# A chunked RWKV-7 scan inside a projection stream: all its products on 64x64 weights, two visits per chunk

## The chip, the cores and the metric

The kernel runs on one core of one Trainium2 chip. The time is the device time of one execution in microseconds (us), the median of several runs. Busy times, waits and clocks come from one profiled execution, which has a time of its own.

## The reference

One layer of a decoder trunk is computed for a prompt of 512 tokens and for 8 sample tokens, 520 columns in all, with width 1024: a half-step SwiGLU, a mixing block with one input projection of 8448 columns, a second half-step SwiGLU, a gated input per layer and a final norm. The part that matters here is the time mixing of the prompt, a delta rule for each of 16 heads with a state of 64x64:

```python
def wkv_step(S, inp):
    r_t, decay_t, k_t, v_t, kk_t, b_t = inp
    sa = jnp.einsum('bhvk,bhk->bhv', S, kk_t)
    S = (S * decay_t[:, :, None, :]
         - sa[..., None] * b_t[:, :, None, :]
         + v_t[..., None] * k_t[:, :, None, :])
    y = jnp.einsum('bhvk,bhk->bhv', S, r_t)
    return S, y
...
z = h @ w_in          # r | k | v | loras | conv B, C, u | merge gates
S_new, ys = lax.scan(wkv_step, S0, (r, decay, k_mod, v, kk, kk * a))
y_A = groupnorm(ys) * gn_w + gn_b + bonus, times the gate
x = x + (sigmoid(g_A) * y_A + sigmoid(g_B) * y_B) @ w_out
```

## The kernel before, in words

Everything is float32. A projection is done as three products per 128x128 weight block (high part times high part, high times low, low times high); line 104 makes the high part of a loaded weight on ScalarE and line 105 the low part on VectorE. The tokens stand in two halves of 260 columns. In the mixing block these products are lines 525 to 527, before and after it lines 114 to 116; "big product" below means one of them.

The time mixing cuts the 512 tokens into 16 chunks of C = 32. For a pair of heads (128 partitions, 64 a head) `stage` makes the tiles AR (decayed keys and queries), BK, the masked scores W, and writes the transposed values into the lower 32 rows of each head's 64 rows of UV (line 772). `invert` inverts a chunk's triangular part in W and folds it into W's upper rows. `scan(q)` then carries the state S through the 16 chunks for two such pairs at once (e = 0 and 1), so it works on four heads; there are four scans, q = 0 to 3, and 64 chunk steps in all. One chunk step is:

- line 889: four products of the state with AR, one for each head, 64x64 weights, into the PSUM tile xy;
- line 894: four products of the values (lower 32 rows of UV) with 32x32 weights from W's lower rows, added to the upper rows of xy;
- line 897: VectorE copies the upper rows of xy into the upper rows of UV, twice 32x128;
- line 906: four products ds of UV with 64x64 weights, the state's increment;
- line 909: VectorE makes the next state from S, the decay lam and ds, two instructions;
- line 874 (`y_part`): four products with 32 columns of weights that complete the output rows of xy; they are issued in the next chunk's first visit, for the chunk before; lines 879 and 882 (`y_out`) then take the output out of PSUM on ScalarE.

A float32 product is two instructions in the trace, so four products are a group of eight records (x8), and each of the four lines has 512 of them. A head sits in partitions 0 to 63 or 64 to 127 (HP), and two products of different halves run side by side.

The chunk steps stand among the big products. A planner at the end of `mix` writes the program: every part is a Python generator, and each `yield a, b` says that a us of TensorE were issued and that b us have to pass before it goes on. Scans, inversions, stages and the output part `fin` take turns with the projections by this planner's clock. After that the framework orders each engine's instructions itself, by readiness, so a group of products need not stay together.

SyncE issues all DMA transfers from one queue, in order: the weights (`raw`, line 97, two buffers), the state out (`out_wkvp`, line 915) and the small tiles of the inversion. An entry that waits holds up those behind it.

Of the kernel before, what the change touches and what calls it, by code (L numbers as in the profile page):

```python
# [8 lines left out]
F32 = mybir.dt.float32  # L9
# [3 lines left out]
ALU = mybir.AluOpType  # L13
AX = mybir.AxisListType

P = 128
# [10 lines left out]
C = 32  # L27
NC = T // C
# [27 lines left out]
def hybrid_step(tc, I, O):  # L56
# [3 lines left out]
    with ExitStack() as top:  # L60
# [299 lines left out]
        with tc.tile_pool(name="mx", bufs=1) as mp:  # L360
            YS = []

            def ysplit(m):
                YS.append(pair(gp, m))
                split(YS, m, YM[m], ALL, nc.vector)
                X[m] = gp.tile([P, N], F32, tag=f"x{m}", name=f"x{m}")
                nc.sync.dma_start(X[m], xd[m])

            def wo_part():

                w = [wprep(I["wo"][m], NT, nc.vector) for m in range(2)]
                ps = [[mmps("wo"), mmps("wo")], [mmps("wo"), pp.tile([P, 512], F32, tag="xy", name="wo", bufs=2)]]
                for k in range(NT):
                    yield ("ys", k)
                    for i in range(2):
                        for j, cs in enumerate(HALF):
                            mm3(ps[i][j], w[i], k, k, YS, cs, k == 0, k == NT - 1)
                    yield 1.3, 0.0
                out.append(ps)

            out = []
            mix(tc, nc, mp, pp, dp, low0, wprep, mwps, mmps, V, VV, I, O, HS, YM, ysplit, wo_part,
                ident, pmask)
# [79 lines left out]
def mix(tc, nc, mp, pp, dp, low0, wprep, mwps, mmps, V, VV, I, O, HS, YM, ysplit, wo_part, ident, pmask):  # L463

    hh, hl = [a for a, _ in HS], [b for _, b in HS]
    v1, act, pool = nc.vector, nc.scalar, nc.gpsimd
# [4 lines left out]
    nc.sync.dma_start(sft, I["sft"])  # L471
    nc.sync.dma_start(cst8, I["cv0"])
    nc.sync.dma_start(smask, I["smask"])
    nsh = mp.tile([P, NZ, B + 1], F32, name="nsh")
    omm = mp.tile([P, NZ], F32, name="omm")
    hka = mp.tile([P, 4, NT], F32, name="hka")
# [19 lines left out]
    HP = (slice(0, 64), slice(64, 128))  # L496
# [5 lines left out]
    def wide(name, shape, bufs=2):  # L502
        return mp.tile([P] + shape, F32, tag=name, name=name, bufs=bufs)
# [129 lines left out]
    mid, both = {}, {}  # L633
# [34 lines left out]
    def stage(p):  # L668
# [39 lines left out]

        if p % 2 == 0:
            both[p // 2] = [wide(n, [NC, 2, 64]) for n in ("AR", "UV")]  # L710
        ar, uv = both[p // 2]
        AR, UV = ar[:, :, p % 2, :].rearrange("p c (s t) -> p c s t", s=2), uv[:, :, p % 2, :]
        W = wide("W", [NC, 128], 4)
# [5 lines left out]
        for cs, ps in zip(GROUPS, kps):  # L719
            for g in range(cs.start, cs.stop, GT):  # L720
                i = g // GT
                for h, hp in enumerate(HP):
                    nc.tensor.matmul(ps[hp, g - cs.start:g - cs.start + GT], rhs=ident[:GT, :GT], start=True, stop=True,
                                     lhsT=rs[:GT, 2 * i + h:2 * i + h + 1].broadcast_to([GT, 64]))
# [21 lines left out]

        dm = dp.tile([2, NC, C, CH], F32, tag="dm", name="dm", bufs=2)
        for h in range(2):
            for b in (0, CH):
                nc.sync.dma_start(dm[h, :, b:b + CH].rearrange("c j t -> j c t"), W[64 * h + b:64 * h + b + CH, :, b:b + CH])  # L750
        for s in range(2):
# [29 lines left out]
    Nz = mp.tile([P, NC, C], F32, name="Nz")  # L781
    pool.memset(F4, 0.0)
    pool.memset(Nz, 0.0)
    CH = C // 2
    UP = (slice(0, C), slice(64, 64 + C))

# [3 lines left out]
    def invert(p):  # L790
# [5 lines left out]
        df = dp.tile([2, NC, C, C], F32, tag="df", name="df", bufs=2)  # L796
        Mr = mp.tile([P, C, CH], F32, tag="Mr", name="Mr")
        for g in range(4):
            nc.sync.dma_start(Mr[32 * g:32 * g + 32], dm.rearrange("h c j t -> (h c) j t"))
        for h in range(2):  # L800
            nc.sync.dma_start(Nz[64 * h:64 * h + CH, :, CH:], W[64 * h:64 * h + CH, :, CH:C])
        yield 0.0, 3.0
        ft = mp.tile([P, 2, 4, CH], F32, tag="ft", name="ft")
        FB, MB = 4 * C + CH, CH * CH
# [51 lines left out]

    def scan(q):

        AR, UV = both[q]
        W, lam, _ = zip(st_out[2 * q], st_out[2 * q + 1])  # L860
        Y = AR
        S, prev = mp.tile([P, 2, 64], F32, tag="S", name="S", bufs=3), None
        pool.memset(S, 0.0)

        def at(ps, rows, e):
            return ps[rows, 64 * e:64 * e + 64]

        def cols(ps, rows):
            return ps[rows, 0:128].rearrange("p (e x) -> p e x", e=2)

        def y_part(c, xy):
            for e in range(2):
                for hp in HP:
                    nc.tensor.matmul(at(xy, slice(hp.start + C, hp.stop), e), lhsT=W[e][hp, c, C:64],  # L874
                                     rhs=UV[hp, c, e, :], start=False, stop=True, skip_group_check=True)

        def y_out(c, xy):
            if c % 2 == 0:
                act.activation(Y[:, c // 2], cols(xy, slice(0, P)), AF.Identity)
            else:  # L880
                for hp in HP:
                    act.activation(Y[hp.start:hp.start + C, c // 2], cols(xy, slice(hp.start + C, hp.stop)), AF.Identity)

        for c in range(NC):
            xy = pp.tile([P, 512], F32, tag="xy", name="xy", bufs=2)
            for e in range(2):

                for hp in HP:
                    nc.tensor.matmul(at(xy, hp, e), lhsT=AR[hp, c, e, :], rhs=S[hp, e, :], start=e == 0, stop=False,  # L889
                                     skip_group_check=True)  # L890
            for e in range(2):
                for h in range(2):
                    up, kp = slice(64 * h, 64 * h + C), slice(64 * h + C, 64 * h + 64)
                    nc.tensor.matmul(at(xy, up, e), lhsT=W[e][kp, c, 0:C], rhs=UV[kp, c, e, :], start=False, stop=True,  # L894
                                     skip_group_check=True)
            for up in (slice(0, C), slice(64, 64 + C)):
                v1.tensor_copy(UV[up, c], cols(xy, up))
            if c:
                y_part(c - 1, prev)
                y_out(c - 1, prev)  # L900
            prev = xy
            yield 0.76, 0.8
            ds = pp.tile([P, 512], F32, tag="us", name="ds")
            for e in range(2):
                for hp in HP:
                    nc.tensor.matmul(at(ds, hp, e), lhsT=W[e][hp, c, 64:], rhs=UV[hp, c, e, :], start=True, stop=True)  # L906
            S1 = mp.tile([P, 2, 64], F32, tag="S", name="S", bufs=3)
            for e in range(2):
                v1.scalar_tensor_tensor(S1[:, e, :], S[:, e, :], lam[e][:, c:c + 1], at(ds, slice(0, P), e),
                                        ALU.mult, ALU.add)  # L910
            S = S1
            yield 0.32, 0.8
        y_part(NC - 1, prev)
        y_out(NC - 1, prev)
        nc.sync.dma_start(O["wkvp"][2 * q:2 * q + 2].rearrange("q p v -> p q v"), S)
        yield 0.2, 0.5

# [116 lines left out]
    def ys(m):  # L1034
# [7 lines left out]
    LAG = 1.2  # L1042
    WIN, DENSE, LIGHT = 8.0, 5500, 0.3
    make = {"scan": scan, "invert": invert, "stage": stage, "fin": fin, "sample": lambda p: sample(),
            "rkv": rkv, "conv": conv, "gate": gate, "low": lowrank, "ys": ys, "wo": lambda p: wo_part()}
    each = lambda kind: [(kind, p) for p in range(NT)]
# [23 lines left out]
    while any(todo.values()) or any(bigs.values()) or live:  # L1070
# [12 lines left out]
        for row in (["big"] if thin and t > 4 else []) + list(todo):  # L1083
            c = live.get(row)
# [115 lines left out]
```

## Time and profile before

| | |
|---|---|
| time, median of 3 runs | 1581.4 us (1580.41 to 1581.67) |
| the profiled execution's own time | 1579.58 us |
| its span, first to last instruction | 1577.8 us |
| TensorE, VectorE, ScalarE, GpSimd busy | 1526.4, 898.7, 552.4, 227.5 us |
| the four scans, from the first product to the last | 78.2, 69.7, 77.5, 89.8 us |
| in them TensorE busy | 77.52, 69.70, 76.45, 84.44 us |
| in them VectorE busy | 54.12, 44.07, 54.17, 62.81 us |

A matmul's busy time overlaps the next one's, so a busy TensorE is not a TensorE at its peak. What a product takes of the engine's time is read from start to start: from the start of one row of the timeline to the start of the next.

### The profile page before, as it was taken

The numbers are of one execution on the slowest core, as the hardware profiler recorded it, in microseconds if no ns is written. First come the engines' busy times: TensorE is split into PE (matmuls) and PEld (weight loads), VectorE is DVE, ScalarE is ACT, GpSimd is POOL, SyncE is SP. The second block draws the span as 40 slices with busy tenths as digits, with TensorE's granted clock in tenths as the row PEclk, the third lists the DMA queues.
The fourth block names the chain that finished last, engine by engine and source line by source line (L and its number), as shares of the span: only waits on it lengthen the run. The fifth ranks groups of instructions, "written<-read, shape, count | busy, mean of one in ns | idle before, by whom it ended". The sixth has DMA issues, their size and how long they took to land. (4 is left out here: it accounts for less than half of the span.)

```text
span 1577.8 us, 35347 instructions
## 1 busy us (share of the span) xinstructions
PE 1526.4 (97%) x15252; PEld 1449.1 (92%) x15252; DVE 898.7 (57%) x1849; ACT 552.4 (35%) x920; POOL 227.5 (14%) x268
## 2 busy tenths in 40 slices
PE   7999999999989999999999998999999999999997
PEld 7999999999989887888887797789999999999997
DVE  7443334433698875757986667765554433443456
ACT  5222122232634342533443252244432212222343
POOL 3111001110222211201320103221011100111001
PEclk9999999999999999999999998999999999999998
DMA  6223222233322211212222221224222322223223
GB/s 206 86 90 108 88 86 91 86 131 116 108 78 74 79 50 47 78 44 60 74 68 56 71 70 64 99 78 150 88 87 94 109 92 72 90 94 120 95 84 105
DMA packets 77532, 140.68 MB, mean 89 GB/s; under 512 B 37512, under 2 KB 42632, under 8 KB 77376
## 3 DMA queue, kind: packets, MB, share of 16 engines
q1 hardware_dynamic: 77376, 138.43, 27.9%
q8 instruction: 119, 1.95, 0.5%
q14 instruction: 37, 0.30, 0.1%
HBM read 127.40 MB, written 10.74 MB: 88 GB/s over the span
## 5 line engine op out<-in xcount | busy, mean ns | idle before, releaser
L114 PE MATMUL big<-xh,hi 128*128 128x260 f32 x1632 | 462.8, 285 | 6.3 <-ACT hi L292 5.2
L115 PE MATMUL big<-xl,hi 128*128 128x260 f32 x1632 | 463.3, 284 | 2.9 <-DVE xl L160 2.9
L116 PE MATMUL big<-xh,lo 128*128 128x260 f32 x1632 | 462.7, 284 | 1.0 <-DVE lo L105 1.0
L104 ACT ACTIVATE hi<-raw 128x1024 fp32r<-128x1024 f32 (+1 forms) x203 | 225.2, 1110 | 624.1 <-PE big L115 292.5
L105 DVE TENSOR_TENSOR lo<-raw,hi 128x1024 fp32r<-128x1024 f32 (+1 forms) x202 | 265.3, 1314 | 98.5 <-ACT hi L104 96.8
L114 PEld LDWEIGHTS big<-xh,hi 128*128 128x128 f32 x1632 | 308.3, 189 | 7.0 <-ACT hi L292 5.2
L525 PE MATMUL big<-xh,hi 128*128 128x260 f32 x1040 | 311.2, 299 | 3.5 <-DVE cu L584 1.6
L115 PEld LDWEIGHTS big<-xl,hi 128*128 128x128 f32 x1632 | 309.0, 189 | 4.1 <-DVE xl L160 4.1
L116 PEld LDWEIGHTS big<-xh,lo 128*128 128x128 f32 x1632 | 308.6, 189 | 1.3 <-DVE lo L105 1.2
L527 PE MATMUL big<-xh,lo 128*128 128x260 f32 x1040 | 300.2, 289 | 2.8 <-DVE lo L105 2.8
L526 PE MATMUL big<-xl,hi 128*128 128x260 f32 x1040 | 301.3, 290 | 0.0
L525 PEld LDWEIGHTS big<-xh,hi 128*128 128x128 f32 x1040 | 197.9, 190 | 16.3 <-DVE k L542 1.6
L527 PEld LDWEIGHTS big<-xh,lo 128*128 128x128 f32 x1040 | 197.0, 190 | 7.4 <-DVE lo L105 3.4
L526 PEld LDWEIGHTS big<-xl,hi 128*128 128x128 f32 x1040 | 198.0, 190 | 5.0
L115 PE MATMUL big<-hl,hi 128*128 128x260 f32 x704 | 199.2, 283 | 1.9 <-POOL hl L249 1.9
L116 PE MATMUL big<-hh,lo 128*128 128x260 f32 x704 | 199.1, 283 | 0.0
L114 PE MATMUL big<-hh,hi 128*128 128x260 f32 x704 | 198.8, 282 | 0.0
L249 POOL TENSOR_TENSOR hl<-u,hh 128x520 fp32r<-128x520 f32 x44 | 70.3, 1599 | 608.2 <-ACT hh L248 608.2
L115 PEld LDWEIGHTS big<-hl,hi 128*128 128x128 f32 x704 | 132.5, 188 | 2.8 <-POOL hl L249 2.8
L114 PEld LDWEIGHTS big<-hh,hi 128*128 128x128 f32 x704 | 132.6, 188 | 0.0
L116 PEld LDWEIGHTS big<-hh,lo 128*128 128x128 f32 x704 | 132.6, 188 | 0.0
L244 DVE TENSOR_TENSOR u<-big,nR 128x260 f32<-128x260 f32 x88 | 37.6, 429 | 127.1 <-PE big L116 127.1
(257 smaller groups left out, 1779.8 us busy)
## 6 DMA issues: line engine op xcount, KB each, us to landing
raw<-in_win SPq DMA_DIRECT2D x66, 512.0 KB, 3.6
raw<-in_wu SPq DMA_DIRECT2D x44, 512.0 KB, 3.5
raw<-in_wd SPq DMA_DIRECT2D x32, 704.0 KB, 4.1
raw<-in_wg SPq DMA_DIRECT2D x43, 512.0 KB, 3.5
raw<-in_wo SPq DMA_DIRECT2D x8, 512.0 KB, 3.5
raw<-in_wpg SPq DMA_DIRECT2D x8, 512.0 KB
x<-in_xT SPq DMA_DIRECT2D x8, 260.0 KB, 5.6
xd<-x SPq DMA_DIRECT2D x8, 260.0 KB, 2.0
```

What stands on the lines that cost most here:

```text
L104: nc.scalar.activation(hi[:, :nk, :], raw[:, :nk, :], AF.Identity)
L105: lo_eng.tensor_tensor(lo[:, :nk, :], raw[:, :nk, :], hi[:, :nk, :].bitcast(F32), ALU.subtract)
L114: nc.tensor.matmul(ps[:, :HN], lhsT=hi[:, wk, :], rhs=x[k][0][:, cs], start=first, stop=False)
L115: nc.tensor.matmul(ps[:, :HN], lhsT=hi[:, wk, :], rhs=x[k][1][:, cs], start=False, stop=False)
L116: nc.tensor.matmul(ps[:, :HN], lhsT=lo[:, wk, :], rhs=x[k][0][:, cs], start=False, stop=last)
L244: nc.vector.tensor_tensor(u1[:, cs], ps, rr[0][:, cs], ALU.mult)
L249: nc.gpsimd.tensor_tensor(hl, u1, hh[:].bitcast(F32), ALU.subtract)
L525: nc.tensor.matmul(ps[:, :HN], lhsT=hi[:, k, :], rhs=hh[k][:, cs], start=k == 0, stop=False)
L526: nc.tensor.matmul(ps[:, :HN], lhsT=hi[:, k, :], rhs=hl[k][:, cs], start=False, stop=False)
L527: nc.tensor.matmul(ps[:, :HN], lhsT=lo[:, k, :], rhs=hh[k][:, cs], start=False, stop=k == nk - 1)
```

## The change

Three things are changed in the scan, and two that they need elsewhere.

```diff
@@ mix, once
+    for h in range(2):
+        v1.tensor_scalar(pmask[64 * h + C:64 * h + 64, C:64], pmask[64 * h + C:64 * h + 64, C:64], 0.5, None, ALU.mult)
@@ stage, once for two head pairs
         if p % 2 == 0:
             both[p // 2] = [wide(n, [NC, 2, 64]) for n in ("AR", "UV")]
+            for up in UP:
+                nc.sync.dma_start(both[p // 2][1][up].rearrange("p c e v -> p (c e v)"), zd)
@@ mix, once: a block of zeros in DRAM
+    zd = dp.tile([C, NC * 128], F32, name="zd")
+    for i in range(NC * 128 // 512):
+        nc.sync.dma_start(zd[:, i * 512:(i + 1) * 512], Nz[0:C].rearrange("p c j -> p (c j)"))
@@ scan
+        def behind(group):
+            for x in group[1:]:
+                tc.add_manual_dep(x.ins, group[0].ins.name, mybir.DependencyInfo(
+                    mybir.DependencyClass.NoSync, mybir.DependencyReason.DATA), reason="order")
         def y_part(c, xy):
-            for e in range(2):
-                for hp in HP:
-                    nc.tensor.matmul(at(xy, slice(hp.start + C, hp.stop), e), lhsT=W[e][hp, c, C:64],
-                                     rhs=UV[hp, c, e, :], start=False, stop=True, skip_group_check=True)
+            return [nc.tensor.matmul(at(xy, hp, e), lhsT=W[e][hp, c, 0:64], rhs=UV[hp, c, e, :], start=False, stop=True,
+                                     skip_group_check=True) for e in range(2) for hp in HP]
         for c in range(NC):
             xy = pp.tile([P, 512], F32, tag="xy", name="xy", bufs=2)
+            group = []
+            for e in (1, 0):
+                for hp in HP:
+                    group.append(nc.tensor.matmul(at(xy, hp, e), lhsT=AR[hp, c, e, :], rhs=S[hp, e, :], start=e == 1,
+                                                  stop=False, skip_group_check=True))
+            behind(group)
             for e in range(2):
                 for hp in HP:
-                    nc.tensor.matmul(at(xy, hp, e), lhsT=AR[hp, c, e, :], rhs=S[hp, e, :], start=e == 0, stop=False,
-                                     skip_group_check=True)
-            for e in range(2):
-                for h in range(2):
-                    up, kp = slice(64 * h, 64 * h + C), slice(64 * h + C, 64 * h + 64)
-                    nc.tensor.matmul(at(xy, up, e), lhsT=W[e][kp, c, 0:C], rhs=UV[kp, c, e, :], start=False, stop=True,
+                    nc.tensor.matmul(at(xy, hp, e), lhsT=W[e][hp, c, 0:64], rhs=UV[hp, c, e, :], start=False, stop=True,
                                      skip_group_check=True)
             for up in (slice(0, C), slice(64, 64 + C)):
                 v1.tensor_copy(UV[up, c], cols(xy, up))
-            if c:
-                y_part(c - 1, prev)
-                y_out(c - 1, prev)
-            prev = xy
-            yield 0.76, 0.8
+            yield 0.55, 0.8
             ds = pp.tile([P, 512], F32, tag="us", name="ds")
+            group = []
             for e in range(2):
-                for hp in HP:
-                    nc.tensor.matmul(at(ds, hp, e), lhsT=W[e][hp, c, 64:], rhs=UV[hp, c, e, :], start=True, stop=True)
+                for hp in HP[::-1]:
+                    group.append(nc.tensor.matmul(at(ds, hp, e), lhsT=W[e][hp, c, 64:], rhs=UV[hp, c, e, :],
+                                                  start=True, stop=True))
+            behind(group + y_part(c, xy))
...
-            yield 0.32, 0.8
-        y_part(NC - 1, prev)
-        y_out(NC - 1, prev)
+            y_out(c, xy)
+            yield 0.6, 0.8
```

The products of line 894 now take all 64 rows and 64 columns; the upper rows of UV are zero at that time (written once for each pair of head pairs by two DMA transfers), so those rows add nothing. The lower rows add to the output rows twice, there and in `y_part`, and the mask of that quarter is halved for it. `y_part` also takes 64 columns, and stands behind ds of its own chunk. `behind` lets no product of a group start before the group's first.

On TensorE, in the first scan, the order before. L889 and L894 make a chunk's first visit, L906 is ds; L525 to L527 are big products; rows are engine order, a trailing x2 is two alike in a row.

```order
L889 MATMUL xy<-S,AR 64x64 x2
L527 MATMUL big<-xh_4192,lo 128x260
L889 MATMUL xy<-S,AR 64x64 x2
L894 MATMUL xy<-UV,W 32x64 x4
L525 MATMUL big<-xh_4194,hi 128x260
L526 MATMUL big<-xl_4195,hi 128x260
L527 MATMUL big<-xh_4194,lo 128x260
L525 MATMUL big<-xh_4196,hi 128x260
L526 MATMUL big<-xl_4197,hi 128x260
L906 MATMUL ds<-UV,W 64x64
L527 MATMUL big<-xh_4196,lo 128x260
L906 MATMUL ds<-UV,W 64x64 x3
```

The state products and ds are each cut in two by a big product; L874's four follow the last row. At the same place of the changed program (L904 was 889, L910 was 894, L919 was 906, L887 was 874; L528 to L530 are the big products):

```order
L904 MATMUL xy<-S,AR 64x64 x4
L910 MATMUL xy<-UV,W 64x64 x4
L529 MATMUL big<-xl_4193,hi 128x260
L530 MATMUL big<-xh_4192,lo 128x260
L528 MATMUL big<-xh_4194,hi 128x260
L529 MATMUL big<-xl_4195,hi 128x260
L530 MATMUL big<-xh_4194,lo 128x260
L528 MATMUL big<-xh_4196,hi 128x260
L529 MATMUL big<-xl_4197,hi 128x260
L919 MATMUL ds<-UV,W 64x64 x4
L887 MATMUL xy<-UV,W 64x64 x4
```

Eight products stand together in each visit, and the output products are those of the same chunk.

On SyncE's queue, where the first scan ends, before: L799 loads a tile of the inversion, L97 a weight, L915 stores the state.

```order
L799 DMA Mr<-dm 32x512 [waits DMAHW1_49]
L97 DMA raw<-in_win 128x1024 [waits DMAHW2_49,DVE_49]
L915 DMA out_wkvp<-S 128x2x64 [waits DMAHW3_49,DVE_49]
L97 DMA raw<-in_win 128x1024 [waits DMAHW4_49,DVE_49]
L665 DMA wdi<-in_wdi 128x128 [waits DMAHW5_49,Pool_49]
```

The same place now:

```order
L97 DMA raw<-in_win 128x1024 [waits DVE_49]
L715 DMA UV<-zd 32x2048 [waits DMAHW3_49,DVE_49,PE_49]
L929 DMA out_wkvp<-S 128x2x64 [waits DMAHW4_49,DVE_49]
L715 DMA UV<-zd 32x2048 [waits DMAHW5_49]
L97 DMA raw<-in_win 128x1024 [waits DMAHW6_49,DVE_49]
```

The two transfers of zeros for the third scan's UV stand around the store of the first scan's state, and the first of them waits for TensorE.

## Rows read from the trace of the kernel before

**Rows 1.** Windows: us; PE, PEld, DVE, ACT, POOL busy (count); clock, DMA, GB/s.
```profile
555.40:633.60 78.20, 77.52 (x1064) 63.04 (x1063) 54.12 (x167) 25.29 (x59) 9.79 (x15) 1.00 0.19 54
942.50:1032.30 89.80, 84.44 (x1040) 68.26 (x1039) 62.81 (x138) 22.50 (x51) 25.46 (x24) 0.94 0.22 72
740.00:780.00 40.00, 37.38 (x398) 34.87 (x397) 37.20 (x103) 20.33 (x39) 12.54 (x16) 0.96 0.21 59
```

**Rows 2.** Timeline, TensorE, a whole chunk: start us, us, engine, line, tiles, count.
```profile
701.58 0.28 PE L527 MATMUL big<-xh,lo 128*128 128x260 f32 x1
701.79 0.45 PE L889 MATMUL xy<-S,AR 64*64 64x64 f32 x8
702.17 0.41 PE L894 MATMUL xy<-UV,W 32*32 32x64 f32 x8
702.51 0.41 PE L874 MATMUL xy<-UV,W 64*32 64x64 f32 x8
702.86 0.39 PE L525 MATMUL big<-xh,hi 128*128 128x260 f32 x1
703.08 0.28 PE L526 MATMUL big<-xl,hi 128*128 128x260 f32 x1
703.20 0.28 PE L527 MATMUL big<-xh,lo 128*128 128x260 f32 x1
...
704.12 0.45 PE L906 MATMUL ds<-UV,W 64*64 64x64 f32 x8
704.50 0.39 PE L525 MATMUL big<-xh,hi 128*128 128x260 f32 x1
```

**Rows 3.** Timeline, TensorE, a chunk cut in four, first scan.
```profile
586.05 0.28 PE L526 MATMUL big<-xl,hi 128*128 128x260 f32 x1
586.27 0.33 PE L889 MATMUL xy<-S,AR 64*64 64x64 f32 x4
586.53 0.38 PE L527 MATMUL big<-xh,lo 128*128 128x260 f32 x1
586.84 0.33 PE L889 MATMUL xy<-S,AR 64*64 64x64 f32 x4
587.10 0.41 PE L894 MATMUL xy<-UV,W 32*32 32x64 f32 x8
587.45 0.39 PE L525 MATMUL big<-xh,hi 128*128 128x260 f32 x1
...
588.03 0.28 PE L526 MATMUL big<-xl,hi 128*128 128x260 f32 x1
588.24 0.32 PE L906 MATMUL ds<-UV,W 64*64 64x64 f32 x2
588.50 0.39 PE L527 MATMUL big<-xh,lo 128*128 128x260 f32 x1
588.81 0.44 PE L906 MATMUL ds<-UV,W 64*64 64x64 f32 x6
589.18 0.41 PE L874 MATMUL xy<-UV,W 64*32 64x64 f32 x8
589.52 0.39 PE L525 MATMUL big<-xh,hi 128*128 128x260 f32 x1
```

**Rows 4.** Timeline, TensorE, 32 products on 64x64 weights in one visit.
```profile
812.89 2.08 PE L741 MATMUL sc<-AR,BK 64*64 64x64 f32 x64
814.90 0.39 PE L525 MATMUL big<-xh,hi 128*128 128x260 f32 x1
```

**Rows 5.** Groups by line: shape xcount | busy us, mean ns | idle before, releaser.
```profile
L897 DVE COPY UV<-xy 32x128 f32<-32x128 f32 x128 | 36.3, 283 | 46.1 <-PE xy L894 43.5
L906 PEld LDWEIGHTS ds<-UV,W 64*64 64x64 f32 x512 | 27.8, 133 | 15.9 <-DVE UV L897 2.4
L894 PEld LDWEIGHTS xy<-UV,W 32*32 32x32 f32 x512 | 16.3, 105 | 4.4
```

**Rows 6.** DMA issues: tile, queue, count, KB each, median us to landing.
```profile
raw<-in_win SPq DMA_DIRECT2D x66, 512.0 KB, 3.6
```

More of the change, by code (lines that the diff above doesn't have):

```diff
@@ L861, in scan @@
         Y = AR
-        S, prev = mp.tile([P, 2, 64], F32, tag="S", name="S", bufs=3), None
+        S = mp.tile([P, 2, 64], F32, tag="S", name="S", bufs=3)
         pool.memset(S, 0.0)
```

## The prediction

> **What bounds the kernel now.** I read first the page's busy shares, then a table of windows over the scans, then the timeline of TensorE around single chunks, and last the groups by line. The page has TensorE busy for nearly the whole span; since a matmul's busy time overlaps the next one's, the windows have to say whether it ever stood still. In the first scan it was busy 77.52 of 78.2 us [rows 1]: nothing that a scan waits for is seen there. Only the fourth scan has holes, 89.80 - 84.44 = 5.4 us, and a mean granted clock of 0.94, so part of it ran at the lower level. VectorE is busy 54.12 of 78.2 us in the first scan, 0.69, and 0.70 in the fourth. So what counts in a scan is what each visit takes of TensorE's time, and that is read from start to start.
>
> **What a visit takes.** The ordinary step from one big product to the next is 0.12 us (703.08 to 703.20) [rows 2]. From the last big product to the first one of a visit it is 0.21, that is 0.09 of entry; the first big product behind a visit holds 0.22, that is 0.10 of exit. Four products on 64x64 weights hold 0.38 (701.79 to 702.17, and again 704.12 to 704.50), four of line 894 hold 0.34 and four of line 874 0.35 [rows 2]. A whole chunk is then 0.09 + 0.38 + 0.34 + 0.35 + 0.10 = 1.26 for the first visit and 0.09 + 0.38 + 0.10 = 0.57 for the second, together 1.83 us.
>
> Many chunks are cut. State products cut 2 and 2: from 586.05 to 587.45 are 1.40 us, less two big steps 1.16, with the exit 1.26 [rows 3]; uncut, the two groups are 0.09 + 0.38 + 0.34 + 0.10 = 0.91. The cut costs 0.35. ds cut 1 and 3: from 588.03 to 589.52 are 1.49, less 0.24 and with the exit 1.35; uncut, ds and line 874 are 0.91. The cut costs 0.44: a single product holds nearly what two do, and each piece pays its entry, its exit and its own start and end.
>
> How often: I counted the program's order. Of 64 groups of state products 28 are cut, of 64 of ds 38; the scan's products stand in 209 runs, where two for each chunk would be 128. The 209 - 128 - 28 - 38 = 15 left over are groups of line 874 that stand alone, at 0.09 + 0.10 = 0.19 each. Before: 64 x 1.83 + 28 x 0.35 + 38 x 0.44 + 15 x 0.19 = 117.1 + 9.8 + 16.7 + 2.9 = 146.5 us of TensorE.
>
> **The changed visits.** No row has eight products in one visit, but 32 of one shape stand in one: they hold 814.90 - 812.89 = 2.01 us [rows 4]. From 4 to 32 products are 28 more for 2.01 - 0.38 = 1.63, so 0.058 each. Eight products hold 0.38 + 4 x 0.058 = 0.61, the visit 0.80 with entry and exit, the chunk 1.60. The bounds: if the two groups of a visit still paid for a change between them, a visit would be 0.91 as ds with line 874; nothing makes it less than 0.57 + 4 x 0.058. I take 0.80, as all eight have the same shape as those of rows 4. In the changed order there are 129 runs, and no state or ds group is cut; two of the others are. After: 128 x 0.80 = 102.4. Removed: 146.5 - 102.4 = **44 us**, of it 14.7 in whole chunks and 29 from the cuts. With 0.91 it would be 30.
>
> The wider weights cost something, and it is inside the 0.80. A load for line 894 has a mean of 105 ns, one for ds 133 [rows 5], 28 ns more for twice the columns; but the step from group to group grows only from 0.34 to 0.38 [rows 2], so a load is mostly hidden behind the product before it, and 128 groups lose 128 x 0.04 = 5 us. A rule of the Trainium skill speaks for more: "TensorE: Matmul & The Clock Gate", LDWEIGHTS, says that a weight load's time goes by its columns and not by its rows. The two means here agree in direction (28 ns for 32 more columns); what it would make of the time if loads set the pace is the third rival below.
>
> **What is added elsewhere**, all at nothing. Two small VectorE operations halve a mask at the start of the mixing block; by the nearest row, the 283 ns copy of the same 32 partitions [rows 5], they would be 0.6 us uncovered; the big products that open the block hide them. Twelve DMA transfers: four write 64 KB of zeros each, eight bring 256 KB into UV. A weight of 512 KB lands in 3.6 us [rows 6] with the DMA engines at 0.19 to 0.22 in the scans [rows 1]. They are on SyncE's queue. Those for the third and the fourth scan wait until TensorE has read UV for the last time in the scan two before; behind them stand weight loads. But they stand beside the store of that scan's last state, which waited for the same chunk and held up the same loads before. The work that hides them is the weight already in the other buffer, 48 big products or 48 x 0.12 = 5.8 us. With that cover gone they cost two late loads, 2 x 3.6 = 7 us. VectorE's and ScalarE's instructions in the scan stay the same in number; the last output products now come with their own chunk.
>
> **What comes back as waits.** A scan is shorter by 11 us in the mean and VectorE has the same work in it: 54.12 us in 78.2 - 11, or 0.81; 62.81 in 89.8 - 11, or 0.80. Each visit waits for VectorE: the second for the two copies (2 x 283 ns), the first for the two halves of the state. Behind a waiting product on TensorE's queue stand the big products, so each wait counts in full. Also, line 874's 0.34 us no longer stand between line 894 and ds, as a cover for the copies. From below: the fourth scan's 5.4 us of holes go. From above: the window 740 to 780, where VectorE is busy 37.20 of 40 us, 0.93, and TensorE lost 40.00 - 37.38 = 2.6 us, or 6.5% [rows 1]; over the four scans, 315 - 44 = 271 us, that is 18 us. The first scan at 0.69 lost 0.7 of 78.2, or 0.9%. A share of 0.81 lies about halfway, but the nearer row is the one at 0.69, and the chunk's steps are spaced as before (nine big products, 1.1 us, between most visits): I take 2%, or 6 us.
>
> **The sum**, against the profiled execution's own 1579.6: 1579.6 - 44 + 6 = 1541.6. The runs' median, 1581.4, lies 1.8 above that execution: **1543 us**. The likeliest case's own range is 1533 to 1554.
>
> **Rivals.**
> *VectorE becomes the bound* of the scans, so that most of the cuts' price only hid its work. For: 0.93 in the window 740 to 780, and more scans than one at 0.8 afterwards. Against: VectorE itself waits 43.5 us for line 894 before its copies [rows 5], so it is more often early than late. It gives back 18 us by the row above, or the whole visits come out at 0.91: 1581.4 - 44 + 18 = 1555, 1581.4 - 30 + 18 = 1569. 1555 to 1570.
> *More than the sum*: the holes of the fourth scan go, and the stretch at the lower clock with them. At 0.94 over 89.8 us the clock was at its lower level, half, for about 2 x 0.06 x 89.8 = 11 us, which cost 5. 1581.4 - 44 - 5 - 5 = 1527. Against: that scan runs beside the sample tokens' state work, which the change leaves where it is.
> *Weight loads set the pace.* As a mechanism of this kernel: each of the 1024 loads of lines 894 and 874 takes 28 ns more [rows 5], and the next product waits for it. 1024 x 0.028 = 29 us, of which 5 are counted: 1543 + 24 = 1567. The 0.34 and 0.38 of rows 2 are against it.
> *Slower: VectorE's queue.* Place: line 897's copies and line 909's updates behind other VectorE work. If at each of the 128 visits one more of its instructions stood ahead (the window 740 to 780 has 37.20 us for 103 of them, 0.36 each [rows 1]) and TensorE had no slack, 46 us would come back, and the time would be level, 1581.4 - 44 + 46 = 1583; with one at the first visits and two at the second, 69 us: 1606. It decides from 44 / 128 = 0.34 us of added wait in the mean. Against: the first scan, where such instructions stood ahead too, lost 0.7 us in 32 visits.
> *The change not doing what it says* is out as far as the order goes: 129 runs.
>
> **Chances.** The forecast 0.62 (1533 to 1554), VectorE the bound 0.20, more than the sum 0.10, weight loads 0.04, slower 0.04. A change of 0.2%, 3 us, is about what this kernel's runs can tell from none. Faster 0.95, the same 0.02, slower 0.03. The range for 8 in 10 is 1530 to 1562: it takes in the likeliest case, half of VectorE as the bound and a part of the case above the sum.
>
> **What would show it.** Visits of eight products that step 0.61 from their first start to the next big product; big products still 0.12; 64 x 2 visits. If a row of the timeline splits in a visit at the change from line 904 to 910, the drain between them was not saved. Scans of about 66, 62, 66 and 75 us; VectorE at 0.8 in them. Waits of lines 919 and 904 for VectorE by a few us together, of big products for a late weight by none. The forecast is wrong if TensorE's holes in the scans are above 15 us, or if a visit holds 0.9.

## The result and the profile after

The changed kernel takes 1537.95 us, the median of 4 runs (1536.35 to 1539.6), beside 1581.54 for the kernel before (1580.41 to 1583.73): ratio 0.9723, 95% interval 0.9706 to 0.974, or 44 us less. The forecast was 1543, with a range of 1530 to 1562.

The first window table of the changed kernel answers [rows 1]: its four scans, then the mixing block in two parts, from the first scan's start to the fourth's, and from there to the block's last big product. The columns are those of [rows 1].

```profile
557.80:622.00 64.20, 63.62 (x1049) 56.31 (x1048) 53.16 (x170) 24.92 (x58) 8.74 (x15) 1.00 0.23 61
661.40:722.80 61.40, 61.33 (x871) 54.95 (x872) 44.19 (x113) 19.30 (x45) 7.79 (x17) 1.00 0.20 59
819.80:883.30 63.50, 62.96 (x1047) 55.81 (x1048) 50.93 (x168) 24.25 (x55) 10.30 (x14) 1.00 0.24 66
916.70:989.40 72.70, 66.23 (x840) 58.34 (x839) 61.68 (x135) 20.22 (x47) 24.72 (x22) 0.95 0.27 90
557.80:916.70 358.90, 348.25 (x5113) 317.83 (x5112) 276.39 (x779) 160.94 (x334) 62.02 (x101) 0.99 0.26 71
916.70:1043.10 126.40, 119.93 (x1330) 111.28 (x1330) 95.54 (x211) 45.28 (x88) 32.91 (x34) 0.97 0.27 88
```

The same two parts of the kernel before:

```profile
555.40:942.50 387.10, 376.62 (x4931) 326.83 (x4930) 277.49 (x779) 158.04 (x329) 59.15 (x100) 1.00 0.23 63
942.50:1086.30 143.80, 136.51 (x1513) 119.37 (x1513) 96.06 (x212) 48.04 (x92) 33.50 (x35) 0.96 0.24 78
```

The first part is 28.2 us shorter, the second 17.4, together 45.6; the first scan starts 2.4 us later (557.8 against 555.4); behind the block both kernels run the same 491.5 us. TensorE stood still (window less busy) for 10.5 + 7.3 = 17.8 us before and for 10.6 + 6.5 = 17.1 now. So nearly all of the gain is time that TensorE was held, and none of it came back as waits. VectorE is busy 0.83 of the first scan and 0.85 of the fourth, where it was 0.69 and 0.70, with nearly the same work in them.

The later start is TensorE's clock. The stretch from 420 us to the first scan, before and now:

```profile
420.00:555.40 135.40, 124.95 (x1496) 118.94 (x1494) 112.85 (x268) 59.13 (x120) 33.17 (x60) 0.99 0.29 81
420.00:557.80 137.80, 128.85 (x1496) 123.00 (x1494) 112.67 (x268) 59.02 (x120) 33.97 (x60) 0.95 0.32 89
```

TensorE has the same 1496 records there and stands still for less (9.0 us against 10.5), but it is busy 3.9 us longer, at a mean granted clock of 0.95 instead of 0.99. In e8 below, which writes no zeros, the clock of this stretch is 0.96 and the scan starts at 557.2, so the zeros are not needed for it; what made the clock fall stays open.

One chunk's first visit in the second scan and the copies and loads, by the timeline and the groups by line, which answer [rows 2] and [rows 5]:

```profile
700.05 0.28 PE L530 MATMUL big<-xh,lo 128*128 128x260 f32 x1
700.26 0.45 PE L904 MATMUL xy<-S,AR 64*64 64x64 f32 x8
700.54 0.40 PE L910 MATMUL xy<-UV,W 64*64 64x64 f32 x8
700.87 0.39 PE L528 MATMUL big<-xh,hi 128*128 128x260 f32 x1
701.10 0.28 PE L529 MATMUL big<-xl,hi 128*128 128x260 f32 x1
```

```profile
L913 DVE COPY UV<-xy 32x128 f32<-32x128 f32 x128 | 36.0, 282 | 31.2 <-PE xy L910 29.8
L910 PEld LDWEIGHTS xy<-UV,W 64*64 64x64 f32 x512 | 21.0, 136 | 0.1
```

The visit holds 700.87 - 700.26 = 0.61 between its edges, as forecast; the step between the two groups is 0.28 where it was 0.38. The exit is 701.10 - 700.87 - 0.12 = 0.11, so the whole visit is 0.81. A load of line 910 takes 136 ns, where one of line 894 took 105, and the visit is as short as forecast all the same. VectorE still waits 29.8 us for line 910 (43.5 before), so it is still early more often than late.

For the experiments I summed, over all 2048 records of the scan's products, the steps from each start to the next start on TensorE, with entries and exits; what a step had above 0.35 us was counted as waiting. This is what the scan *holds*: 149.0 us before, 104.7 after, 44.3 less. How an entry or an exit beside another small product is counted can move one sum by 1 to 2 us and a difference of two by about 1. Beside it stand the runs of scan products in each program's order, the groups of state products and of ds that are cut in it, and what TensorE stood still in the two parts of the block, with the second part's granted clock.

| kernel | runs | cut | ratio (95%) | holds | still, 1st + 2nd part | clock |
|---|---|---|---|---|---|---|
| before | 209 | 28, 38 | 1 | 149.0 | 10.5 + 7.3 | 0.96 |
| after | 129 | 0, 0 | 0.9723 (0.9706 to 0.9740) | 104.7 | 10.6 + 6.5 | 0.97 |
| e1 before, kept together | 131 | 1, 1 | 0.9873 (0.9855 to 0.9891) | 120.0 | 13.0 + 9.9 | 0.93 |
| e2 after, first ready | 180 | 24, 29 | 0.9833 (0.9812 to 0.9854) | 126.4 | 11.5 + 4.3 | 0.97 |
| e3 values on 32 rows | 128 | 0, 0 | 0.9748 (0.9727 to 0.9768) | 111.8 | 9.7 + 6.2 | 0.99 |
| e4 outputs on 32 columns | 129 | 1, 0 | 0.9819 (0.9804 to 0.9834) | 112.1 | 9.5 + 12.2 | 0.94 |
| e5 outputs in next visit | 137 | 2, 1 | 0.9745 (0.9721 to 0.9769) | 109.8 | 10.4 + 7.5 | 0.95 |
| e6 copies twice | 124 | 0, 0 | 0.9858 (0.9837 to 0.9879) | 107.7 | 14.2 + 16.3 | 0.90 |
| e7 planned 0.8 | 131 | 0, 1 | 0.9745 (0.9727 to 0.9764) | 106.9 | 12.2 + 6.6 | 0.96 |
| e8 as e3, no zeros | 128 | 0, 0 | 0.9769 (0.9747 to 0.9790) | 113.0 | 9.9 + 6.1 | 0.96 |
| e9 one operation on GpSimd | 129 | 0, 0 | 0.9710 (0.9690 to 0.9730) | 103.8 | 10.6 + 7.3 | 0.99 |
| e10 as e4, three scans | 131 | 1, 0 | 0.9737 (0.9719 to 0.9755) | 109.1 | 9.7 + 5.5 | 0.99 |
| e11 two on GpSimd | 129 | 0, 0 | 0.9754 (0.9734 to 0.9773) | 105.6 | 10.8 + 13.4 | 0.97 |
| e12 after again | 129 | 0, 0 | 0.9706 (0.9685 to 0.9727) | 104.2 | 10.9 + 6.2 | 0.99 |

The kernel before took 1584 to 1585 us beside e1 to e12, so they are compared by their ratios; 0.001 is 1.6 us.

### The profile page after: what moved, and what is told of

Same layout as the page of the kernel before. It is cut to its first block, busy times and chain, and to the rows that moved or that the text cites. A ratio compares the mean times of both kernels' runs of the same rounds, so it can differ in the third digit from the quotient of the medians.

```text
span 1534.6 us, 35437 instructions
## 1 busy us (share of the span) xinstructions
PE 1484.7 (97%) x15252; PEld 1435.5 (94%) x15252; DVE 897.3 (58%) x1851; ACT 552.5 (36%) x920; POOL 230.9 (15%) x269
## 4 chain that ended last, share of the span: by engine, by line
PE 47%; DVE 5%; issue 2%; ACT 1%; POOL 1%; DMA 0%; DVEq 0%; POOLq 0%; ACTq 0%; SPq 0%
PE big L115 10%; PE big L114 10%; PE big L116 10%; PE big L528 4%; PE big L530 4%; PE big L529 4%; PE xy L904 1%; PE ds L919 1%; DVE lo L105 1%; PE xy L910 1%; PE xy L887 1%; PE sc L746 0%; DVE fo L457 0%; PE ft L856 0%; ACT hi L104 0%
## 5 line engine op out<-in xcount | busy, mean ns | idle before, releaser
L528 PE MATMUL big<-xh,hi 128*128 128x260 f32 x1040 | 310.3, 298 | 1.7 <-ACT cc L580 1.0
L530 PE MATMUL big<-xh,lo 128*128 128x260 f32 x1040 | 299.6, 289 | 2.0 <-DVE lo L105 2.0
L528 PEld LDWEIGHTS big<-xh,hi 128*128 128x128 f32 x1040 | 199.8, 192 | 11.4 <-ACT cc L580 1.2
L530 PEld LDWEIGHTS big<-xh,lo 128*128 128x128 f32 x1040 | 199.2, 192 | 4.2 <-DVE lo L105 2.3
```

The costliest lines, as they stand in the source:

```text
L528: nc.tensor.matmul(ps[:, :HN], lhsT=hi[:, k, :], rhs=hh[k][:, cs], start=k == 0, stop=False)
L530: nc.tensor.matmul(ps[:, :HN], lhsT=lo[:, k, :], rhs=hh[k][:, cs], start=False, stop=k == nk - 1)
```

## The experiments

**Cuts alone.** e1 is the kernel before with the changed order inside a group:

```diff
-            for e in range(2):
+            group = []
+            for e in (1, 0):
                 for hp in HP:
-                    nc.tensor.matmul(at(xy, hp, e), lhsT=AR[hp, c, e, :], rhs=S[hp, e, :], start=e == 0, ...)
+                    group.append(nc.tensor.matmul(at(xy, hp, e), lhsT=AR[hp, c, e, :], rhs=S[hp, e, :], start=e == 1, ...))
...
-                for hp in HP:
-                    nc.tensor.matmul(at(ds, hp, e), ...)
+                for hp in HP[::-1]:
+                    group.append(nc.tensor.matmul(at(ds, hp, e), ...))
+            behind(group)
```

(The first visit's group also takes in the products of the values and the output products; that is left out here.)

> The kernel before, with its narrow weights and its output products in the next chunk's first visit, but with the order that keeps a visit together: the group that needs two VectorE results begins with the product that needs the last one. In its order 131 runs of scan products instead of 209, 1 group of state products and 1 of ds cut instead of 28 and 38. If the cuts cost what the prediction's working says (28 x 0.35 + 38 x 0.44 + 15 x 0.19 = 29 us): 1581.5 - 29 = 1552. If a cut only moved waiting time about, so that what is saved comes back as waits for VectorE: 1570 or above. If all of the gain is the shapes': 1581.

Measured 1564.9, ratio 0.9873, 20 us less. The scan holds 29.0 us less, as expected, but 9 came back by the runs, and 12 in the profiled executions, where the block takes 513.7 us instead of 530.9. TensorE stands still 2.5 us longer in the first part and 2.6 in the second, and the clock fell to 0.99 and 0.93. The lower level is half of the upper one, so a window in which TensorE works all the time loses its length times what its mean clock lacks to 1. As an estimate from these rows that is 0.07 x 140.3 - 0.04 x 143.8 = 4 us more in the second part, and up to 4 (0.01 x 373.4) in the first. Its two parts:

```profile
553.80:927.20 373.40, 360.40 (x4929) 320.09 (x4928) 277.56 (x779) 158.19 (x329) 58.81 (x100) 0.99 0.23 65
927.20:1067.50 140.30, 130.40 (x1513) 118.03 (x1513) 96.90 (x211) 48.12 (x92) 33.58 (x35) 0.93 0.25 80
```

The cuts are most of the price (29 of the 44 us), and what their absence gives may come back in part.

**The old order in the new shapes.** e2 is the changed kernel with the order turned back, `behind` kept:

```diff
-            for e in (1, 0):
+            for e in range(2):
...
-                for hp in HP[::-1]:
+                for hp in HP:
```

> The changed kernel with the products of a group in the old order (e = 0 and the lower half first), the groups' added dependencies kept. In its order 180 runs, 24 groups of state products and 29 of ds are cut again; shapes, zeros and the place of the output products as changed. If the cuts are what costs: 24 x 0.35 + 29 x 0.44 = 21 us back, 1538 + 21 = 1559. If the change of shapes is what brought the time: 1538 to 1543.

Measured 0.9833, 17 to 20 us above the changed kernel; the scan holds 21.7 more, as expected. One of its cuts in the timeline: a single ds product holds 580.91 - 580.66 = 0.25, and the other three the rest of their visit.

```profile
580.45 0.28 PE L530 MATMUL big<-xh,lo 128*128 128x260 f32 x1
580.66 0.33 PE L919 MATMUL ds<-UV,W 64*64 64x64 f32 x2
580.91 0.39 PE L528 MATMUL big<-xh,hi 128*128 128x260 f32 x1
581.23 0.38 PE L919 MATMUL ds<-UV,W 64*64 64x64 f32 x5
```

So `behind` doesn't keep a visit whole. The changed program without it has the same order on every engine, row for row (so it wasn't run), and with it the old order is cut all the same. What keeps it whole is which product stands first, since that is all that e2 changes: now it is the one that needs VectorE's last result. The reason is read from the program and not measured: the group then becomes ready all at once; before, the first product was ready one VectorE instruction ahead of the rest and was put in.

**Rows and columns.** e3 gives the products of the values 32 rows and 64 columns, e4 the output products 64 rows and 32 columns; e10 is e4 in the first three scans alone.

```diff
# e3
-                    nc.tensor.matmul(at(xy, hp, e), lhsT=W[e][hp, c, 0:64], rhs=UV[hp, c, e, :], ...)
+                    kp = slice(hp.start + C, hp.stop)
+                    nc.tensor.matmul(at(xy, hp, e), lhsT=W[e][kp, c, 0:64], rhs=UV[kp, c, e, :], ...)
# e4 (e10: n = C if q < 3 else 0)
-            return [nc.tensor.matmul(at(xy, hp, e), lhsT=W[e][hp, c, 0:64], ...
+            return [nc.tensor.matmul(at(xy, slice(hp.start + C, hp.stop), e), lhsT=W[e][hp, c, C:64], ...
```

> The changed kernel with the products of the values on 32 rows and 64 columns of weights instead of 64 and 64; the zeros are then not needed, but still written; visits stay together (128 runs). If any change of shape inside a visit has the engine drained: the first visit holds 0.91 instead of 0.81, 64 x 0.10 = 6.5 us, 1544.5. If only a change of the columns does: first visits at 0.81 and 1538, and the 64 rows and zeros were not needed.

> The changed kernel with the output products on 64 rows and 32 columns of weights, behind ds in its visit as now. If any change of shape drains: the second visit holds 0.91 instead of 0.81, 64 x 0.10 = 6.5 us, 1544.5. If only a change of the rows does: 1538. With the kernel of 32 rows and 64 columns it tells apart which of the two numbers counts.

> The kernel with output products on 32 columns (ratio 0.982, 8 us more than the drain's price), but only in the first three scans; the fourth has the changed kernel's 64x64. If the drain's price is right, 0.10 at each of 48 second visits, and the rest came from VectorE's lateness beside the sample tokens in the fourth scan: 4.8 us above the changed kernel, ratio 0.9755. If a change of columns costs more than its rows show wherever it stands: three quarters of 15, 11 us above, ratio 0.979.

Both hold 7 us more (111.8 and 112.1 against 104.7). A visit of each, with its step from group to group 0.38 instead of 0.28, e3 first:

```profile
705.63 0.45 PE L904 MATMUL xy<-S,AR 64*64 64x64 f32 x8
706.01 0.45 PE L911 MATMUL xy<-UV,W 32*64 32x64 f32 x8
706.38 0.39 PE L528 MATMUL big<-xh,hi 128*128 128x260 f32 x1
```

```profile
703.58 0.45 PE L919 MATMUL ds<-UV,W 64*64 64x64 f32 x8
703.96 0.41 PE L887 MATMUL xy<-UV,W 64*32 64x64 f32 x8
704.30 0.39 PE L528 MATMUL big<-xh,hi 128*128 128x260 f32 x1
```

Either number changing costs the step, so the zeros and the 64 rows are needed. The Trainium skill has the rule, "TensorEngine Tiling (Array Packing)", Key Properties: "Changing tiling mode (not just tile) drains the TensorE". These rows agree and put about 0.1 us to it.

e3 came out 4 to 7 us above the changed kernel, as expected, e4 15 to 18. The fourth scan's part of e4 and the longest waits of TensorE in it (engine, line, waited for: us, times, longest) say more:

```profile
925.90:1063.20 137.30, 125.15 (x1330) 114.91 (x1330) 97.71 (x211) 41.76 (x84) 32.22 (x34) 0.94 0.24 80
```

```profile
PE ds L919 <- DVE UV L913: 5.7, 4, 1.6
...
PE big L530 <- DVE lo L105: 5.1, 3, 4.0
```

VectorE had fallen behind there. This part is 10.9 us longer than the changed kernel's: 4.6 of them in the fourth scan (925.9 to 1003.2, 77.3 us against 72.7) and 6.3 behind its last product, where at 1006.6 one weight's low part came 4.0 us late. e10, with the same price in three scans and the changed kernel's products in the fourth, holds 4.9 us more than e12, for 4.8 expected. Its ratio is 0.0031 or 4.9 us above e12's, but only 0.0014 or 2.2 us above the changed kernel's first one, so the time agrees with the price without fixing it. e4's other 8 to 11 us go with the narrow output products in the fourth scan; which of the changes in the order they come from isn't shown.

**The place of the output products.** e5 puts them back into the next chunk's first visit, on 64x64 weights:

```diff
+            if c:
+                group += y_part(c - 1, prev)
+                y_out(c - 1, prev)
+            behind(group)
```

> The changed kernel with the output products back in the next chunk's first visit, as 64x64 weights: a visit of twelve and one of four products instead of eight and eight. In its order 137 runs, 4 groups of all kinds cut. By the price of a visit nothing changes: first visits 0.80 + 4 x 0.058 = 1.03, second ones 0.57, together 1.60, four runs more at 0.19 and the cuts 2 us: 1540. If the place of the output products behind ds is what saves time (a cover for the state's update, or the output leaving PSUM earlier), it is slower by 5 us or more: 1543 or above.

Measured 1543.1, 0.9745, 4 to 6 us above, of it 5 in what the scan holds: its 8 additional runs and its cuts, more than the 2 us expected. Standing still is 17.8 against 17.1. The place as such is worth little, but this doesn't separate it from the cuts that come with it.

**How much room VectorE has.** e6 does each copy twice:

```diff
-                v1.tensor_copy(UV[up, c], cols(xy, up))
+                for _ in range(2):
+                    v1.tensor_copy(UV[up, c], cols(xy, up))
```

> The changed kernel with each of the 128 copies of line 913 done twice: 128 x 0.283 = 36 us more of VectorE, all in the scans, 0.57 us more between a first and a second visit. If VectorE has room beside nine big products (1.07 + 0.15 of the visit's end + 0.09 of entry, against 0.86 for the wait and the copies): 1.43 instead of 0.86 is 0.12 above the 1.31 of cover, at 64 visits 8 us: 1546. If VectorE is nearly the bound of the scans, as the second case of the prediction has it, half of it or more comes through: 1556 to 1574. If its queue is full of room: 1538.

Measured 0.9858, 21 to 24 us above: of 36 us more VectorE some 60% come through. The first three scans took it with 3.6 us of standing still, the fourth's part stood 9.8 us longer and at a clock of 0.90, which is 142.3 x 0.10 = 14 us against 4:

```profile
560.70:926.60 365.90, 351.71 (x5114) 319.32 (x5113) 299.12 (x875) 159.10 (x331) 59.30 (x101) 0.99 0.25 69
926.60:1068.90 142.30, 126.00 (x1333) 116.38 (x1330) 110.23 (x244) 48.04 (x90) 31.63 (x34) 0.90 0.25 78
```

VectorE is busy 22.7 us longer than in the changed kernel in the first part and 14.7 in the second. So it had room in three scans and hardly any in the fourth, beside the sample tokens' state.

**The zeros.** e8 is e3 without them: the two `dma_start` lines of the change left out.

> The kernel with values on 32 rows and 64 columns (1546 at a kernel before of 1585, ratio 0.975), without the twelve transfers of zeros, which it doesn't need. If they cost nothing, as the prediction has it: ratio 0.975 again, within 0.002. If they hold up weight loads or small tiles of the inversion on SyncE's queue (up to 7 us by the prediction's bound): 0.970 to 0.973.

Measured 0.9769, no less than e3's 0.9748 (the intervals overlap). The transfers cost nothing that can be told, which with these intervals means less than about 3 us. By the changed kernel's issues they land in 3.6 us, and a weight of the block in 3.9 instead of 3.6 [rows 6]; but with the same zeros a weight lands in 3.6 in e4, e6, e7 and e10, and without them in 3.7 in e8, so the 0.3 are not theirs.

```profile
raw<-in_win SPq DMA_DIRECT2D x66, 512.0 KB, 3.9
UV<-zd SPq DMA_DIRECT2D x8, 256.0 KB, 3.6
```

**Attempts at the fourth scan.** e9 and e11 move the sample state's subtraction, and the addition too, to GpSimd; e7 tells the planner 0.8 us a visit; e12 is the changed kernel again.

```diff
-            v1.tensor_tensor(S, S, t, ALU.subtract)
+            pool.tensor_tensor(S, S, t, ALU.subtract)      # e9, e11
-            v1.tensor_tensor(S, S, t, ALU.add)
+            pool.tensor_tensor(S, S, t, ALU.add)           # e11
```

```diff
-            yield 0.55, 0.8
+            yield 0.8, 0.8                                 # e7
...
-            yield 0.6, 0.8
+            yield 0.8, 0.8
```

> The changed kernel with one of the five VectorE operations of a step of the sample tokens' state (the subtraction, 8 x 0.68 = 5.5 us) on GpSimd. In the fourth scan TensorE stands still for 7.4 us, since these operations stand between the scan's copies and updates on VectorE. If that is the cause of the holes, 3 to 5 us go: 1533 to 1535, ratio 0.970. If GpSimd's longer operation (1.1 to 1.5 us) only makes VectorE wait for it at the addition that follows, with the scan's copies behind: 1538 or above.

> The changed kernel with two of the five VectorE operations of a step of the sample tokens' state on GpSimd, the subtraction and the addition, so that VectorE no longer waits for GpSimd between them. 16 x 0.68 = 11 us less on VectorE, nearly all in the fourth scan. If VectorE is what stands in the way there: the 7 us of holes go, and the lower clock in them: 1530 to 1534, ratio 0.968. If the holes come from the chain of the scan itself: 1537, ratio 0.972, as with one operation moved.

> The changed kernel with the planner told 0.8 us for each visit, what the trace shows, instead of 0.55 and 0.60; the scans then stand wider apart among the other work. If waits for VectorE are a matter of how many big products stand between two visits: fewer of them, 3 to 5 us less, 1533 to 1535, ratio 0.970. If what follows a scan (output part, merge gates) then comes too late: 1540 or more, ratio 0.974 or more.

> The changed kernel once more, unchanged, beside the three others on the same chip, since kernels before of 1581 to 1585 stand beside the runs so far. Ratio 0.9723 within 0.002. If the earlier ratio was the luck of its runs, it is 0.975 or more, as with the values on 32 rows.

e9 is level with the changed kernel (0.9710 against 0.9723 and 0.9706); its expected 3 to 5 us didn't come, the second part stands still for 7.3 instead of 6.5. e11 is slower, 0.9754: VectorE has 5 us less to do in the fourth scan's part (90.66 against 95.54), and now waits for GpSimd ahead of the scan's own copies. By its waits, and by VectorE's timeline at the longest of them:

```profile
DVE sT L1013 <- POOL sS L1012: 11.7, 6, 3.4
...
PE xy L904 <- DVE S L924: 6.2, 5, 2.4
PE ds L919 <- DVE UV L913: 5.2, 2, 4.0
```

```profile
928.43 1.73 DVE L1013 TENSOR_TENSOR sT<-sS,sv 128x512 f32<-128x512 f32 x1 [3.40 <-POOL sS L1012]
930.09 0.27 DVE L913 COPY UV<-xy 32x128 f32<-32x128 f32 x1
930.29 0.66 DVE L1014 TENSOR_REDUCE ys<-sT 128x8 f32<-128x512 f32 x1
930.96 0.29 DVE L913 COPY UV<-xy 32x128 f32<-32x128 f32 x1
```

VectorE sat idle 3.40 us for GpSimd with the scan's two copies behind, and ds on TensorE waited 3.95 us for them, until 931.40. So the holes aren't VectorE's amount of work alone: here an instruction that waits at the head of its queue kept the scan's next copies waiting. e7 is slower too, 0.9745: TensorE stands still for 12.2 instead of 10.6 us in the first part, and the scan holds 2.2 more. None of the three beats the changed kernel.

## Why the prediction was right, and where not

*The visit's price* was right: 44 us forecast, 44.3 in the sum of steps, with the eight products at 0.61 as worked out and the visit at 0.81 for 0.80. Both of its levels were 2 to 3 us low (146.5 for 149.0, 102.4 for 104.7), which the difference doesn't feel. The two parts of it hold too: cuts 29 (e1: 29.0; e2: 21.7 for 21), the rest from the shapes (e3, e4: 7 each).

*The waits that come back* are the term that was mis-sized: 6 us forecast, and measured 0.6 more in the four scans (7.1 to 7.7 us of standing still) and 0.7 less in the whole block. I took 2% of the scans, between a stretch with VectorE at 0.69 and one at 0.93. VectorE went to 0.83 and TensorE lost 0.6 us in the first scan where it had lost 0.7. The share was the wrong gauge: as these rows suggest, the nine big products between visits cover a VectorE that is busy but in time. Without that term the forecast would have been 1537, beside 1538 measured; but that nearness is in part luck, since the later start, 2.4 us of clock, was in no term. In the profiled executions the three terms, 44.3 + 0.7 - 2.4, make 42.6 of the 43.2 us that were gained.

*VectorE as the bound* of 1555 to 1570 did not come, but e6 shows how near it is in the fourth scan, and e1 and e4 lost about 9 us each to waits and the clock, e4 nearly all of it from the fourth scan on. Which program gets off is a matter of its order; what in the order decides it stays open.

*Weight loads as the pace* fell: 136 ns a load and a visit of 0.81 all the same. *VectorE's queue making it slower* fell as well. *More than the sum*: the fourth scan's part kept its holes (6.5 us); its clock was 0.97 in the first profile and 0.99 in e12's, so that stretch differs between two executions of one program. *The zeros at nothing* held, to about 3 us.

*What keeps a visit together* was in no term, and the order shows that it isn't the dependencies.

## What to carry to other kernels

Price a small product by the step from start to start, with what it costs to enter and to leave its shape, and count in the program's order how often it is paid; the differences of that sum came within 1 us in six of these kernels, and 3 us off in e5. Where a scheduler orders by readiness, put first the product of a group whose operand comes last, so that the group becomes ready at once. Before filling the other engine's idle time, look whether its waits reach the busy one; its share of busy time alone did not tell that here.

## What the runs showed of the hardware

A change of only the rows (64 to 32) or only the columns of the weights costs the step between groups as much as a change of both: 0.38 us for four products against 0.28 without a change (e3, e4, the changed kernel). One float32 product alone holds 0.25 us (e2), four hold 0.38 [rows 2]. In the changed kernel's fourth scan no hole of TensorE was longer than 1.1 us, and the granted clock still fell to its lower level, half, at a run of three, of 0.6, 1.0 and 1.1 us between 958 and 963 us: 0.95 over that scan. In e6, with holes up to 3.6 us, it was 0.90 over the second part.
